# Hybrid decoder block on one core: the second matmul of the indexer scores contracts over all 128 partitions instead of 64

## The chip, the core and the metric

The kernel runs on one core of one Trainium2 chip. The metric is device time in microseconds (us), the median over runs of the whole program. A core has a matrix engine (PE, which loads a stationary operand, recorded as PEld, and then streams a moving operand past it), a vector engine (DVE), a scalar engine (ACT), GpSimd (POOL) and a sync engine (SP) that here issues most DMAs.

## The reference

One decoder layer on 256 tokens plus 16 learned meta tokens, width 1024, all in float32. Cut to what the change touches:

```python
proj = rmsnorm(h, norm_mix_g) @ w_in          # split into q, k, v, qi, ki, wi, cu, cb, cc, ga, gb
...
rel   = relu(einsum('bthd,bsd->bths', qi_b, k_idx))            # 8 index heads, each 64 wide
score = einsum('bths,bth->bts', rel, w_b * IDX_SCALE)
score = where(visible, score, -inf)
_, sel = top_k(score, topk)                                     # 68 keys for each token
...                                                             # attention over the selected keys
y_conv = (cb * short_conv(cc * cu, conv_w)) @ w_conv_out
mixed  = sigmoid(ga) * y_attn + sigmoid(gb) * y_conv
h = h + mixed @ w_out
...                                                             # SwiGLU FFN, final norm
```

The index scores only choose keys: `rel` for 8 heads, weighted and added up, then the top 68.

## The kernel before

**Numbers in two parts.** Every float32 operand of a matmul is split into a high part in the PE's reduced float32 format and a low part, the rest. A product is made of three terms: high by high, high by low and low by high. ACT makes the high part of a weight block (`whi`, line 137), DVE the low part (`wlo`, line 145).

**Weights.** The weights come as 160 blocks of 128 x 1024 in the order in which they are used (`UNITS`); each is loaded, split some four blocks ahead (`ahead`), and multiplied by one of two helpers. `narrow` makes three matmuls for each of 8 slices of a block (lines 214 to 216, 256 to 272 columns). `product` makes two for each slice: one of 512 columns that takes the high weights by high and low activations at once (line 250), and one of 256 for the low weights (line 253). Both write to a PSUM buffer named `acc`, of which there are four.

**Index scores.** The index queries of a head are 64 wide. `indexer_queries` puts the high part of head 2j into partitions 0 to 63 and its low part into 64 to 127 of `qi`; for head 2j+1 the high part is in 64 to 127 and the low part in 0 to 63. The keys' high part `ki.hi` and low part `ki.lo` stand in both halves of the partitions. A score of one head is then two matmuls into a `misc` buffer (four of these): one over 128 partitions that adds high by high and low by high, and one over the 64 partitions where the high part of the query stands, by the keys' low part. `scores` is called for 2 blocks of 128 tokens by 8 heads, 16 times in all: 8 times with 144 columns (the keys that the first token block can see) and 8 times with 272. After each, ACT applies relu (line 306) and DVE adds the weighted result up (lines 310 and 312).

**Order.** The order on every engine is that of the code. `some_scores` takes two scores at a time and is called after the matmuls of the short convolution's blocks (`cu`, `cb`, `cc`): eight groups of two scores, that is of four matmuls, each between two weight blocks. Then the eight attention heads follow, whose `logits` (line 370) are made with the same three-pass helper of 144 and 272 columns, into `misc` buffers too, over 128 partitions throughout. In the rows, `qi` goes by the name of its buffer, `big`, and the attention's q and k by `q_hi`, `q_lo`, `k_hi`, `k_lo`.

Of the kernel before, what the change touches and what calls it, by code (L numbers as in the profile page):

```python
# [25 lines left out]
DI = 64  # L26
# [42 lines left out]
def program(nc, tc, h_in, params, weights, out):  # L69
# [14 lines left out]
    mm = nc.tensor.matmul  # L84
# [3 lines left out]
    def bank():  # L88
        return acc.tile([P, 512], F32, name="acc")

    def side():
        return misc.tile([P, 512], F32, name="misc")

    def temp(n=L):
        t = ring.tile([P, L], F32, name="temp")
        return t[:, 0:n]
# [121 lines left out]
    def narrow(i, src, c0=0, late=False):  # L218
        n = src.hi.shape[2]
        o = bank()[:, 0:n - c0]  # L220
        hi, lo = got.pop(i)
        w = lambda k: slice(k * P, k * P + P)
        for k in range(KT):
            xh, xl = src.hi[:, k, c0:n], src.lo[:, k, c0:n]
            if late:
                mm(o, hi[:, w(k)], xh, start=k == 0, stop=False)
                mm(o, hi[:, w(k)], xl, start=False, stop=False)
            else:
                three_passes(o, hi[:, w(k)], lo[:, w(k)], xh, xl, k == 0, k == KT - 1)
        if late:  # L230
            for k in range(KT):
                mm(o, lo[:, w(k)], src.hi[:, k, c0:n], start=False, stop=k == KT - 1)
        return o
# [21 lines left out]
    def product(i, src, c0=0):  # L255
        o = bank()
        hi, lo = got.pop(i)
        w = lambda k: slice(k * P, k * P + P)
        for k in range(KT - 1):
            wide_high(o, hi[:, w(k)], src, k, c0, start=k == 0, stop=False)  # L260
            wide_low(o, lo[:, w(k)], src, k, c0, start=False, stop=False)
        k = KT - 1
        wide_low(o, lo[:, w(k)], src, k, c0, start=False, stop=False)
        wide_high(o, hi[:, w(k)], src, k, c0, start=False, stop=True)
        return o

    bias = one.tile([P, OFF[1] + L], F32, name="bias")
    qi = one.tile([P, NI, S], R, name="big2")
# [3 lines left out]
    ki = Pair(one, [P, L], "ki")  # L272
# [25 lines left out]
    def scores(t, head):  # L298
        n = SEEN[t]
        o = side()  # L300
        c = slice(t * P, t * P + P)
        rows = slice((head % 2) * DI, (head % 2) * DI + DI)
        mm(o[:, 0:n], qi[:, head, c], ki.hi[:, 0:n], start=True, stop=False)  # L303
        mm(o[:, 0:n], qi[rows, head, c], ki.lo[rows, 0:n], start=False, stop=True)  # L304
        r = temp(n)
        act(r, o[:, 0:n], AF.Relu)
        s = sc[:, OFF[t]:OFF[t] + n]
        w = wsc[:, t, head:head + 1]
        if head == 0:
            V.tensor_scalar(s, r, w, None, op0=OP.mult)  # L310
        else:
            V.scalar_tensor_tensor(s, r, w, s, op0=OP.mult, op1=OP.add)
# [209 lines left out]
    def some_scores():  # L522
        for _ in range(2):
            if tasks:
                t, head = tasks.pop(0)
                scores(t, head)
                if head == NI - 1:
                    causal(t)
                    steps.extend([topk_steps(t)] * (-(-TOPK // 8) + 1))
# [45 lines left out]
    o = narrow(0, uT, late=True)  # L575
# [3 lines left out]
    last, o = o, narrow(1, uT, late=True)  # L579
# [4 lines left out]
    last, o = o, narrow(2, uT)  # L584
# [3 lines left out]
    last, o = o, narrow(3, uT)  # L588
# [3 lines left out]
    for i in range(4, LEAD):  # L592
        last, o = o, narrow(i, uT)
# [5 lines left out]
        n = LEAD - 4  # L599
# [28 lines left out]
    for j in range(KT):  # L628
        i = first["wo"] + j
        ahead(i)  # L630
        o = product(i, mix()) if j < KT - 1 else narrow(i, mix())
# [31 lines left out]
    for j in range(KT):  # L663
        o = bank()
# [36 lines left out]
    for n in range(2):  # L701
        c = slice(n * 512, n * 512 + 512)
# [53 lines left out]
```

## Time and profile before

| | |
|---|---|
| median of 3 runs | 504.36 us (504.21 to 505.34) |
| span of the profiled execution | 502.3 us |
| its own time beside its span | not listed apart; the median is 2.06 us above the span |
| PE busy | 492.7 us, 98% of the span |
| PE weight loads (PEld) busy | 444.5 us, 88% |
| DVE, ACT, POOL busy | 72%, 60%, 15% |
| mean granted PE clock | 0.998 of full |

The span reaches from the first to the last instruction. PE and PEld are the same engine: a load of the next stationary operand can run under a matmul. Matmuls are pipelined and their ends are modelled, so durations of neighbours overlap; the distance from the start of one to the start of the next is what a matmul takes of the engine.

### The profile page before, as it was taken

What the parts mean: (1) busy time and instruction counts of PE and PEld (TensorE: products, weight loads), DVE (VectorE), ACT (ScalarE), POOL (GpSimd) and SP (SyncE); (2) the same over time, 40 slices, a digit from 0 to 9 for tenths busy, and PEclk for the clock granted to TensorE, in tenths of its full rate; (3) what the DMA queues carried; (4) which work ended last, traced back from release to release, by engine and by line L of the source; (5) the groups of instructions that cost most, each with busy time, mean ns of one, the idle gap of its engine ahead of it and who ended that gap; (6) DMA issues with size and microseconds to landing.
All of it is one profiled execution on the core that took longest, in us unless ns stands there. A gap on an engine that the chain in (4) does not pass through costs nothing.

```text
span 502.3 us, 8349 instructions
## 1 busy us (share of the span) xinstructions
PE 492.7 (98%) x3157; PEld 444.5 (88%) x3157; DVE 362.7 (72%) x661; ACT 301.9 (60%) x567; POOL 73.3 (15%) x75
## 2 busy tenths in 40 slices
PE   8999999999999999999999999999999999999995
PEld 6988889999999999888888989888888888888895
DVE  5898678886677777587776797778777777764521
ACT  6685566655577777765656465666666656553511
POOL 3451112211000000000000012121221122000110
PEclk9999999999999999999999999999999999999999
DMA  8847335556434544365556475456656565665002
GB/s 311 322 129 251 127 127 185 193 169 215 163 127 127 159 135 133 124 204 197 182 176 201 133 246 176 155 187 201 203 178 197 173 196 182 206 204 177 1 0 85
DMA packets 24376, 86.09 MB, mean 171 GB/s; under 512 B 2832, under 2 KB 2832, under 8 KB 24336
## 3 DMA queue, kind: packets, MB, share of 16 engines
q1 hardware_dynamic: 24192, 85.54, 51.6%
q8 instruction: 25, 0.41, 0.3%
q14 instruction: 15, 0.12, 0.1%
q10 hardware_dynamic: 144, 0.02, 0.0%
HBM read 84.50 MB, written 1.05 MB: 170 GB/s over the span
## 4 chain that ended last, share of the span: by engine, by line
PE 90%; issue 3%; DVE 2%; ACT 1%; DMA 1%; POOL 1%; SPq 0%; POOLq 0%; DVEq 0%
PE acc L250 42%; PE acc L253 21%; PE acc L214 7%; PE acc L215 7%; PE acc L216 7%; DMA h_all<-in_h_in_dram 1%; PE misc L304 1%; DVE aT L566 1%; PE misc L303 1%; PE misc L410 1%; ACT temp L555 0%; PE misc L427 0%; PE misc L216 0%; POOL rt L201 0%; PE misc L214 0%
## 5 line engine op out<-in xcount | busy, mean ns | idle before, releaser
L250 PE MATMUL acc<-aT,whi 128*128 128x512 f32 x576 | 202.7, 399 | 0.0
L145 DVE TENSOR_TENSOR wlo<-raw,whi 128x1024 fp32r<-128x1024 f32 x158 | 192.8, 1225 | 7.0 <-ACT whi L137 4.8
L137 ACT ACTIVATE whi<-raw 128x1024 fp32r<-128x1024 f32 x158 | 163.8, 1047 | 0.4 <-PE acc L250 0.3
L253 PE MATMUL acc<-aT,wlo 128*128 128x256 f32 x576 | 150.1, 281 | 0.0
L250 PEld LDWEIGHTS acc<-aT,whi 128*128 128x128 f32 x576 | 105.3, 188 | 19.7
L250 PE MATMUL acc<-big,whi 128*128 128x512 f32 x330 | 115.2, 394 | 0.0
L253 PEld LDWEIGHTS acc<-aT,wlo 128*128 128x128 f32 x576 | 108.8, 189 | 5.7
L253 PE MATMUL acc<-big,wlo 128*128 128x256 f32 x330 | 88.4, 282 | 0.0
L215 PE MATMUL acc<-aT,whi 128*128 128x272 f32 (+2 forms) x272 | 78.1, 287 | 1.1 <-DVE aT L566 1.1
L214 PE MATMUL acc<-aT,whi 128*128 128x272 f32 (+2 forms) x272 | 78.6, 289 | 0.0
L216 PE MATMUL acc<-aT,wlo 128*128 128x272 f32 (+2 forms) x272 | 77.6, 285 | 0.0
L246 DVE TENSOR_TENSOR temp<-acc,temp 128x256 f32<-128x256 f32 x87 | 36.9, 424 | 49.8 <-ACT temp L245 49.8
L250 PEld LDWEIGHTS acc<-big,whi 128*128 128x128 f32 x330 | 60.6, 188 | 11.9
L253 PEld LDWEIGHTS acc<-big,wlo 128*128 128x128 f32 x330 | 62.0, 188 | 2.5
L215 PEld LDWEIGHTS acc<-aT,whi 128*128 128x128 f32 x272 | 51.3, 189 | 1.8 <-DVE aT L566 1.3
L214 PEld LDWEIGHTS acc<-aT,whi 128*128 128x128 f32 x272 | 51.4, 189 | 0.7
L216 PEld LDWEIGHTS acc<-aT,wlo 128*128 128x128 f32 x272 | 51.2, 188 | 0.0
L119 ACT ACTIVATE big<-temp 128x256 fp32r<-128x256 f32 x45 | 18.8, 418 | 47.0 <-DVE temp L660 23.2
L623 POOL TENSOR_TENSOR sq_sum<-sq_sum,temp 128x256 f32<-128x256 f32 x12 | 11.0, 918 | 236.6 <-ACT temp L620 236.6
L245 ACT ACTIVATE temp<-acc 128x256 f32<-128x256 f32 x87 | 32.7, 376 | 13.9 <-PE acc L250 11.5
L656 POOL TENSOR_TENSOR temp<-temp,rstd 128x256 f32<-128x256 f32 x22 | 26.0, 1182 | 93.9 <-ACT temp L655 93.9
L239 DVE TENSOR_TENSOR h_all<-h_all,acc 128x256 f32<-128x256 f32 x16 | 6.7, 416 | 28.6 <-PE acc L250 21.7
(162 smaller groups left out, 529.5 us busy)
## 6 DMA issues: line engine op xcount, KB each, us to landing
raw<-in_weights_dram SPq DMA_DIRECT2D x158, 512.0 KB, 3.5
h_all<-in_h_in_dram SPq DMA_DIRECT2D x4, 272.0 KB, 4.6
out_dram<-big SPq DMA_DIRECT2D x4, 256.0 KB, 2.3
raw<-in_weights_dram SPq DMA_DIRECT2D x2, 256.0 KB, 3.8
par<-in_params_dram ACTq DMA_DIRECT2D x1, 24.0 KB, 3.3
```

Source lines behind the costliest of these rows:

```text
L119: act(hi, src, AF.Copy)
L137: act(high[i], raw[i], AF.Copy)
L145: V.tensor_sub(lo, raw.pop(i), high[i].bitcast(F32))
L214: mm(o, wh, xh, start=first, stop=False)
L215: mm(o, wh, xl, start=False, stop=False)
L216: mm(o, wl, xh, start=False, stop=last)
L245: act(t, o[:, S:2 * S], AF.Copy)
L246: V.tensor_tensor(t, o[:, 0:S], t, OP.add)
L250: mm(halves(o), w, src.both[:, k, :, c0:c0 + S], **kw)
L253: mm(o[:, 0:S], w, src.hi[:, k, c0:c0 + S], **kw)
L623: G.tensor_tensor(sq_sum, sq_sum, sq, OP.add)
L656: G.tensor_tensor(s, s, rstd, OP.mult)
```

## The change

The second matmul of a score takes all 128 partitions: the stationary operand is now the whole `qi[:, head, c]` (query high and low part), and the moving one the keys' low part in both halves. The result gains the term low by low, which was left out before. The stationary operand is then the same as that of the first matmul of the pair. Nothing else changes: on every engine the list of instructions, their order and their semaphore waits are the same as before.

```diff
@@ -299,9 +299,8 @@
         n = SEEN[t]
         o = side()
         c = slice(t * P, t * P + P)
-        rows = slice((head % 2) * DI, (head % 2) * DI + DI)
         mm(o[:, 0:n], qi[:, head, c], ki.hi[:, 0:n], start=True, stop=False)
-        mm(o[:, 0:n], qi[rows, head, c], ki.lo[rows, 0:n], start=False, stop=True)
+        mm(o[:, 0:n], qi[:, head, c], ki.lo[:, 0:n], start=False, stop=True)
         r = temp(n)
         act(r, o[:, 0:n], AF.Relu)
         s = sc[:, OFF[t]:OFF[t] + n]
```

## Rows read from the trace of the kernel before

**Rows 1.** The page: busy us, share, instructions; the chain that ended last, by engine.

```profile
PE 492.7 (98%) x3157; PEld 444.5 (88%) x3157; DVE 362.7 (72%) x661; ACT 301.9 (60%) x567; POOL 73.3 (15%) x75
...
PE 90%; issue 3%; DVE 2%; ACT 1%; DMA 1%; POOL 1%; SPq 0%; POOLq 0%; DVEq 0%
```

**Rows 2.** What PE waited for from 34 to 480 us: total, times, longest.

```profile
PE acc L215 <- DVE aT L566: 1.1, 1, 1.1
```

**Rows 3.** Windows: length, busy us of PE, PEld, DVE, ACT, POOL, granted clock, DMA.

```profile
20.00:35.00 15.00, 13.51 (x111) 13.06 (x110) 12.87 (x21) 10.39 (x17) 10.38 (x9) 1.00 0.49 158
41.50:71.00 29.50, 29.50 (x180) 24.75 (x179) 20.83 (x45) 17.38 (x37) 5.43 (x7) 1.00 0.47 160
71.00:120.00 49.00, 49.00 (x370) 47.28 (x370) 42.49 (x95) 30.16 (x55) 11.91 (x12) 1.00 0.55 175
```

**Rows 4.** Line 304 on PE: min/median/max ns, first and last start us, forms.

```profile
L304 PE MATMUL misc<-ki_lo,big x16: 330/359/389, 41.9 to 70.7; 64*128 64x144 f32 x8, 64*128 64x272 f32 x8
```

**Rows 5.** Timeline of PE, a group of scores with 144 columns: start us, us.

```profile
45.65 0.23 PE L303 MATMUL misc<-ki_hi,big 128*128 128x144 f32 x1
45.81 0.33 PE L304 MATMUL misc<-ki_lo,big 64*128 64x144 f32 x1
46.07 0.34 PE L303 MATMUL misc<-ki_hi,big 128*128 128x144 f32 x1
...
46.59 0.39 PE L214 MATMUL acc<-aT,whi 128*128 128x258 f32 x1
46.82 0.29 PE L215 MATMUL acc<-aT,whi 128*128 128x258 f32 x1
46.94 0.29 PE L216 MATMUL acc<-aT,wlo 128*128 128x258 f32 x1
```

**Rows 6.** Timeline of PE, a group of scores with 272 columns.

```profile
57.39 0.28 PE L303 MATMUL misc<-ki_hi,big 128*128 128x272 f32 x1
57.60 0.39 PE L304 MATMUL misc<-ki_lo,big 64*128 64x272 f32 x1
57.92 0.39 PE L303 MATMUL misc<-ki_hi,big 128*128 128x272 f32 x1
...
58.56 0.39 PE L214 MATMUL acc<-aT,whi 128*128 128x258 f32 x1
58.78 0.28 PE L215 MATMUL acc<-aT,whi 128*128 128x258 f32 x1
```

**Rows 7.** Timeline of PE, the logits of one attention head.

```profile
125.97 0.23 PE L214 MATMUL misc<-k_hi,q_hi 128*128 128x144 f32 x1
126.04 0.27 PE L215 MATMUL misc<-k_lo,q_hi 128*128 128x144 f32 x1
126.15 0.27 PE L216 MATMUL misc<-k_hi,q_lo 128*128 128x144 f32 x1
126.26 0.33 PE L214 MATMUL misc<-k_hi,q_hi 128*128 128x272 f32 x1
126.43 0.28 PE L215 MATMUL misc<-k_lo,q_hi 128*128 128x272 f32 x1
126.55 0.29 PE L216 MATMUL misc<-k_hi,q_lo 128*128 128x272 f32 x1
126.67 0.27 PE L394 MATMUL misc<-ident,temp 128*128 128x128 f32 x1
```

**Rows 8.** Timeline of the weight loads, at the scores and at the logits.

```profile
45.80 0.18 PEld L304 LDWEIGHTS misc<-ki_lo,big 64*128 64x128 f32 x1 [0.20 <-issue]
46.07 0.19 PEld L303 LDWEIGHTS misc<-ki_hi,big 128*128 128x128 f32 x1
...
125.97 0.19 PEld L215 LDWEIGHTS misc<-k_lo,q_hi 128*128 128x128 f32 x1
```

**Rows 9.** Timelines of DVE and PE: the 88th `wlo` (first of two), and its first use.

```profile
286.28 2.35 DVE L145 TENSOR_TENSOR wlo<-raw,whi 128x1024 fp32r<-128x1024 f32 x2
...
293.05 0.28 PE L253 MATMUL acc<-big,wlo 128*128 128x256 f32 x1
```

## The prediction

> **What bounds the kernel now.** I read the page first: PE is busy for 98% of the span, and the chain that ended last runs over PE for 90% of it [rows 1]. A busy PE row alone proves little, because the records of neighbouring matmuls overlap; so next I asked what PE waited for. From 34 us to 480 us there is one such wait, 1.1 us in all, and it belongs to the first units after the input norm [rows 2]. After it PE goes from matmul to matmul without a gap: in the stretch with the index scores, 41.5 to 71 us, it is busy for all of its 29.5 us, and in the stretch behind it for all of 49 us, at the full granted clock [rows 3]. So in this kernel the time from one matmul's start to the next one's start is time on the path, wherever it stands before 480 us, as long as the weights keep coming.
>
> The changed matmul is the 64-partition one of the scores: 16 of them, 8 of 144 columns and 8 of 272 [rows 4], all between 41.9 and 71 us. They come in eight groups of four matmuls (303, 304, 303, 304), four groups of each width.
>
> **What a group costs now.** I read starts, not durations. In a group of 144 columns the first matmul starts at 45.65, and then come 45.81, 46.07, and the next weight block's first matmul at 46.59: steps of 0.16, 0.26, and 0.52 for the last two, so 0.26 each. That first matmul of the next block again takes 0.23 until 46.82, while its twins after it take 0.12 [rows 5]. From 45.65 to 46.82 it is 1.17 us. In a group of 272 columns the steps are 0.21, 0.32, then 0.64 for two, and 0.22 for the next block's first: 57.39 to 58.78 is 1.39 us [rows 6].
>
> These steps are not the price of streaming. The difference between the two widths, 128 columns, costs 0.32 - 0.26 = 0.06 us; about 0.2 us of each step remains that no column explains. Nor is PE waiting for another engine there [rows 2]. What it does show is a load that cannot be prepared: the 64-row load of line 304 begins at 45.80, when its matmul begins at 45.81, after 0.20 us of idle on the load side, and the 128-row load after it begins at 46.07, again only with its own matmul [rows 8, 5]. So both directions, 128 to 64 rows and back, put load, stream and a gap one behind the other.
>
> **What a group will cost.** The trace of before holds the same thing without a change of height: the logits of one head, three matmuls of 144 and three of 272 columns, into the same kind of buffer, with the same stationary operand twice in a row, 128 rows throughout. There the load of the second matmul begins at 125.97, exactly when the first one starts streaming [rows 7, 8]. The starts go 125.97, 126.04, 126.15, 126.26, then for 272 columns 126.43, 126.55, and 126.67 for what follows [rows 7]: 0.70 us for six. That divides into 0.11 for each of 144 columns (0.07, which only says that the first load was ready, then 0.11 and 0.11) and 0.125 for each of 272, since 3 x 0.11 + 3 x 0.125 = 0.705. After the change all four matmuls of a group are of this kind, and the next block's first matmul takes its usual 0.12 [rows 5].
>
> - 144 columns: 4 x 0.11 + 0.12 = 0.56 instead of 1.17, 0.61 saved in a group.
> - 272 columns: 4 x 0.125 + 0.12 = 0.62 instead of 1.39, 0.77 saved.
> - Eight groups: 4 x 0.61 + 4 x 0.77 = 5.5 us.
>
> Three of the groups are followed by a `product`, whose first matmul has 512 columns instead of some 258; its own excess I take to be the same 0.11. The first group, whose 64-row matmuls begin at 41.9 [rows 4], follows two small transposes, and its first load may still come late; that is one step of at most 0.26 - 0.11 = 0.15 that may not be saved, which I leave in the range.
>
> **What is not saved or added.** The number of instructions is the same on every engine, loads included, so nothing is gained from the fact that a pair now uses one stationary operand twice; the logits show such a pair reloading it. The added contraction over 64 more partitions costs no columns. The matmul reads the second half of `ki_lo` too, but the waits on every engine are the same as before.
>
> **Where the saving could stop.** It reaches the end only if the weights are there 5.5 us earlier. The thinnest cushion that I found after 42 us is at the 88th `wlo`: the first of two that begin at 286.28 takes some 1.2, about half of 2.35, so it ends at 287.5, and PE first uses it at 293.05 [rows 9]: 5.55 us. It does not have to give all of that up, since DVE works behind PE in program order and moves forward with it. In the score stretch itself DVE has 20.83 us of work [rows 3]; in 29.5 - 5.5 = 24.0 us that is 87% busy, which is just what it is in the stretch behind, 42.49 of 49 us [rows 3], where PE never waits. ACT would have 17.38 of 24.0, 72%. So I let the whole 5.5 us through. The page's own time beside the span is not given; the median stands 2.06 us above the span of 502.3, and I take that as fixed: span 496.8, time 504.36 - 5.5 = **498.9 us**.
>
> **Bounds of the step.** The nearest rows give an interval for a step after the change: for 144 columns 0.07 (the logits' first) to 0.16 (the step from 303 to 304 now, its load being ready), for 272 columns 0.12 to 0.21 [rows 5 to 7]. The cheap end makes a group 4 x 0.07 + 0.12 = 0.40 and 4 x 0.12 + 0.12 = 0.60, and saves 4 x (1.17 - 0.40) + 4 x (1.39 - 0.60) = 6.2 us, 498.1; the dear end makes it 0.76 and 0.96 and saves 4 x (1.17 - 0.76) + 4 x (1.39 - 0.96) = 3.4 us, 501.0. I stand at 0.11 and 0.125, since the logits match in rows, columns, buffer and repeated operand.
>
> **Rivals.**
>
> *Loads stop hiding.* If a 128-row load could not run under a 128-row matmul, a step would be load plus stream: 0.11 + 0.06 = 0.17 for 144 columns (0.06 is what 128 columns cost above), and 0.11 + 0.12 = 0.23 for 272. Against the 1.17 and 1.39, with the usual 0.12 behind, that saves 4 x (1.17 - 0.80) + 4 x (1.39 - 1.04) = 2.9 us: 501.5. The logits' loads speak against it [rows 8], and so does the usual step of 0.12 [rows 5], which is shorter than such a sum. The Trainium skill states this rule: its page "TensorE: Matmul & The Clock Gate", section "Part 3: Packing small matmuls — row/col tiling", says that weight loads overlap with matmuls in flight only when their row groups differ, and its closing table advises cutting contractions of under 128 into row groups, which is what the old matmul did and the new one undoes. By that rule the time would be the 501.5 just given; the trace does not agree, since a 128-row load begins at 125.97 under a 128-row matmul that starts at 125.97. Chance 2%.
>
> *The feed gives part of it back.* If DVE or the loads of weights have less room than I read, PE meets a wait after 71 us and loses between 1 and 5 of the 5.5: 500 to 504. The cushion of 5.55 us and the 87% speak against it; chance 6%, two thirds of it still faster by more than 0.2%.
>
> *The height is not the cause.* If the 0.2 us hang on something else that the scores have and the logits lack (two matmuls to a buffer instead of three to half of one, or `qi` as the stationary operand), the steps remain and so does the time, 504.4. For the height speaks that line 303 behind 304 is as late as 304 itself though it is a plain 128-row matmul. Chance 3%.
>
> *Slower: a wait that lowers the clock.* If PE, being earlier, ran dry for so long that its clock fell to the lower level, each weight block would take twice as long. A block of 24 matmuls at 0.12 [rows 5] takes 2.9 us and would lose as much, so from two such blocks on (5.8 us) the change loses. Against it: from 20 to 35 us PE was idle for 1.5 of 15 us, and the granted clock stayed at 1.00, the 2.4 GHz level [rows 3]. Chance 2%.
>
> **How the numbers follow.** The likeliest case keeps 87%. A change under 0.2%, about 1 us, could not be told from none by a measurement of this kernel. Faster by more than that: 87 + 2 + 4 = 93%; within it: the 3% of the third rival and 2% of the second, 5%; slower: 2%. The range is that of the step's bounds, 498.1 to 501.0, opened by 0.1 at the low end for the spread of runs; it leaves out the rivals and little else.
>
> **What would show it.** In the profile after, the second matmul of a score stands as 128*128; the steps in a group are 0.11 to 0.13, its load begins with the matmul before it, and the block behind a group has no long first step. The stretch from the first score to the last shrinks by about 5 us, relu on ACT waits for PE less, and every later stage stands 5.5 us earlier with no new wait of PE. I am wrong in the size if the steps stay near 0.16 and 0.21, wrong in the cause if they stay at 0.26 and 0.32, and wrong about the path if the steps shrink but PE then waits for `wlo` or `whi` after 71 us.

## The result and the profile after

| | before | after |
|---|---|---|
| median, all runs compared | 504.85 us (504.21 to 505.34, 4 runs) | 498.64 us (498.46 to 499.88, 4 runs) |
| ratio to before, 95% interval | | 0.9886 [0.9867, 0.9905] |
| span of the profiled execution | 502.3 us | 496.8 us |

The forecast was 498.9 us, with a span of 496.8 us. The interval of the ratio puts the gain between 4.8 and 6.7 us. The runs of before fall into two bands (504.2 to 504.4, and 505.3) and one of the changed kernel's lies 1.2 us above its other three, so the 6.2 us between the medians mixes bands; within the lower band the difference is 5.7 us, within the upper one 5.5.

The page of the changed kernel, its line of busy times, which answers to [rows 1]:

```profile
PE 487.0 (98%) x3157; PEld 442.7 (89%) x3157; DVE 362.3 (73%) x661; ACT 300.3 (60%) x567; POOL 73.4 (15%) x75
```

PE does as many matmuls and loads as before, and is still busy for 98% of a span that is 5.5 us shorter. The other engines' work is what it was. The five waits of PE that its view lists over the whole span are single ones, as before; this is one of the two longest, which answers to [rows 2] (none of the other four is in the score stretch):

```profile
PE acc L215 <- DVE aT L565: 1.1, 1, 1.1
```

No wait is new; two of the others grew by 0.3 us each, and one shrank by 0.2. Windows of the same kernel, columns as in [rows 3], the score stretch and 49 us of the stretch behind:

```profile
41.50:66.40 24.90, 24.90 (x186) 23.68 (x186) 20.61 (x45) 15.02 (x36) 4.20 (x6) 1.00 0.58 191
...
71.00:120.00 49.00, 49.00 (x370) 47.29 (x370) 42.06 (x91) 30.83 (x56) 11.15 (x10) 1.00 0.59 186
```

In the score stretch PEld's share rises from 24.75 of 29.5 to 23.68 of 24.9 us: the time in which no load ran falls from 4.75 to 1.2 us. (This window reaches a little further into the block behind, which is why it holds 186 matmuls and not 180; over the whole span the loads are as many as before.) The stretch behind is as full as it was.

The ends of the score stretch, its first matmul and the second one of the block behind the last group, in the kernel before (with the second score matmul) and in the changed one, whose first score matmul, at 41.88, stands among the lines of the small transposes below:

```profile
41.68 0.33 PE L303 MATMUL misc<-ki_hi,big 128*128 128x144 f32 x1
41.95 0.33 PE L304 MATMUL misc<-ki_lo,big 64*128 64x144 f32 x1
...
71.21 0.28 PE L215 MATMUL acc<-aT,whi 128*128 128x258 f32 x1
```

```profile
65.86 0.28 PE L215 MATMUL acc<-aT,whi 128*128 128x258 f32 x1
```

It takes 65.86 - 41.88 = 23.98 us instead of 71.21 - 41.68 = 29.53, which is 5.55 us less.

Timeline of PE in the changed kernel, a group of 144 columns and a group of 272, to be laid beside [rows 5, 6] (the lines after the removed one have moved up by one, so 302 and 303 are the former 303 and 304):

```profile
45.25 0.23 PE L302 MATMUL misc<-ki_hi,big 128*128 128x144 f32 x1
45.31 0.28 PE L303 MATMUL misc<-ki_lo,big 128*128 128x144 f32 x1
45.42 0.28 PE L302 MATMUL misc<-ki_hi,big 128*128 128x144 f32 x1
45.53 0.28 PE L303 MATMUL misc<-ki_lo,big 128*128 128x144 f32 x1
45.65 0.33 PE L214 MATMUL acc<-aT,whi 128*128 128x258 f32 x1
45.81 0.28 PE L215 MATMUL acc<-aT,whi 128*128 128x258 f32 x1
...
55.16 0.29 PE L302 MATMUL misc<-ki_hi,big 128*128 128x272 f32 x1
55.28 0.29 PE L303 MATMUL misc<-ki_lo,big 128*128 128x272 f32 x1
55.41 0.29 PE L302 MATMUL misc<-ki_hi,big 128*128 128x272 f32 x1
55.53 0.29 PE L303 MATMUL misc<-ki_lo,big 128*128 128x272 f32 x1
55.66 0.28 PE L214 MATMUL acc<-aT,whi 128*128 128x258 f32 x1
55.78 0.29 PE L215 MATMUL acc<-aT,whi 128*128 128x258 f32 x1
```

From the group's first matmul to the second one of the next block it is 45.81 - 45.25 = 0.56 us instead of 1.17, and 55.78 - 55.16 = 0.62 instead of 1.39. The weight loads show why; a load of the first group:

```profile
45.25 0.19 PEld L303 LDWEIGHTS misc<-ki_lo,big 128*128 128x128 f32 x1
```

Line 303's load begins at 45.25, with the matmul ahead of it, and not with its own as at 45.80 in [rows 8].

### The profile page after: what moved, and what is told of

The parts are those of the page before. It is cut to its first block, busy times and chain, and to the rows that moved or that the text cites. A ratio compares the mean times of both kernels' runs of the same rounds, so it can differ in the third digit from the quotient of the medians.

```text
span 496.8 us, 8349 instructions
## 1 busy us (share of the span) xinstructions
PE 487.0 (98%) x3157; PEld 442.7 (89%) x3157; DVE 362.3 (73%) x661; ACT 300.3 (60%) x567; POOL 73.4 (15%) x75
## 4 chain that ended last, share of the span: by engine, by line
PE 90%; issue 3%; DVE 2%; ACT 1%; DMA 1%; POOL 1%; SPq 0%; POOLq 0%; DVEq 0%
PE acc L250 42%; PE acc L253 22%; PE acc L215 7%; PE acc L216 7%; PE acc L214 7%; DMA h_all<-in_h_in_dram 1%; DVE aT L565 1%; PE misc L409 1%; ACT temp L554 0%; PE misc L426 0%; PE misc L302 0%; POOL rt L201 0%; PE misc L214 0%; ACT whi L137 0%; PE misc L216 0%
```

## The experiments

Times of these runs stand beside runs of the kernel before on the same chip: 504.79 us (504.03 to 505.62, 13 runs) for the first three and for that with the same matmul elsewhere, 504.45 us (503.86 to 505.76, 13 runs) for the other three. The nine profiled executions also differ for a reason outside the scores. In four of them (before, changed, the first two experiments) the first score matmul begins between 41.5 and 41.9 us, and the mean granted clock of PE from 8 to 16 us is 1.00; in the other five it begins between 42.2 and 42.7, and that clock is 0.79, with 0.50, the 1.2 GHz level, from 11 to 12 us. In all nine PE is busy for only 0.38 to 0.43 us of the one from 8 to 9. So the group lengths of the traces decide where a time alone would not.

**Half as many changes of height, as many 64-row matmuls.** On the kernel before:

```diff
-        mm(o[:, 0:n], qi[:, head, c], ki.hi[:, 0:n], start=True, stop=False)
-        mm(o[:, 0:n], qi[rows, head, c], ki.lo[rows, 0:n], start=False, stop=True)
+        os = [side() for _ in heads]
+        for o, head in zip(os, heads):
+            mm(o[:, 0:n], qi[:, head, c], ki.hi[:, 0:n], start=True, stop=False)
+        for o, head in zip(os, heads):
+            rows = slice((head % 2) * DI, (head % 2) * DI + DI)
+            mm(o[:, 0:n], qi[rows, head, c], ki.lo[rows, 0:n], start=False, stop=True)
...
```

> The kernel before, with the four matmuls of a group reordered: both heads' 128-row matmuls first, then both heads' 64-row matmuls. As many 64-row matmuls as before (16), half as many changes of height (2 in a group instead of 4). Theory, the price hangs on a change of height: before a group cost 0.61 (144 columns) or 0.77 us (272) more than without any change, so 0.15 or 0.19 for each change; two of them are saved in each of eight groups, 4 x 0.31 + 4 x 0.39 = 2.8 us, which makes 502 us where the kernel before takes 504.4 to 504.9. Rival, the price hangs on each 64-row matmul (its load or its stream is slow): 16 of them remain, the time stays at that of the kernel before. Second rival, two 64-row matmuls in different halves of the array run at the same time: then the second one costs next to nothing and the gain is up to 0.12 us in a group larger, 501 us.

Measured 500.69 us (500.12 to 501.47), ratio 0.9920 [0.9905, 0.9936]. Timeline of PE, a group of 272 columns:

```profile
55.56 0.41 PE L303 MATMUL misc<-ki_hi,big 128*128 128x272 f32 x2
55.90 0.39 PE L306 MATMUL misc<-ki_lo,big 64*128 64x272 f32 x2
56.22 0.39 PE L214 MATMUL acc<-aT,whi 128*128 128x258 f32 x1
56.44 0.28 PE L215 MATMUL acc<-aT,whi 128*128 128x258 f32 x1
```

Its loads of 64 rows:

```profile
55.90 0.19 PEld L306 LDWEIGHTS misc<-ki_lo,big 64*128 64x128 f32 x2
```

The group takes 56.44 - 55.56 = 0.88 us instead of 1.39. The 16 matmuls of 64 rows are all there, so the price does not hang on each of them; the first rival falls. The second one is also seen: both 64-row matmuls together take 56.22 - 55.90 = 0.32 us, the step that a single one took in [rows 6]. One lies in partitions 0 to 63, the other in 64 to 127, and they run at once: both records fit into the 0.39 us, and both loads into the 0.19 us, that one alone takes. So of the 0.51 us that the group saves, 0.12 is this and 0.39 the two changes of height, 0.19 each, as the theory had it. The Trainium skill's page "TensorEngine Tiling (Array Packing)", section "Key Properties", says both things, that different tiles run in parallel and that a change of the tiling mode drains the engine; it gives no price. The trace agrees with the first; for the second it shows a price at each change, but not that this is a drain.

**Another stationary operand.** On the changed kernel:

```diff
-        mm(o[:, 0:n], qi[:, head, c], ki.lo[:, 0:n], start=False, stop=True)
+        mm(o[:, 0:n], qi[:, (head + 1) % NI, c], ki.lo[:, 0:n], start=False, stop=True)
```

> The changed kernel, but the second matmul of a pair takes the query of the next head as its stationary operand, over 128 partitions, so that the two matmuls of a pair no longer share one. It computes another low term than the reference's. Theory, the height alone matters: as the changed kernel, 498.6 us, steps of 0.11 and 0.125 us in a group. Rival, the gain comes from using one stationary operand twice: the steps grow by the part that this gave, up to the 0.26 and 0.32 of before, and the time goes up to 504 us.

Measured 499.12 us (498.39 to 499.36), ratio 0.9886 [0.9871, 0.9900]. Timeline of PE, a group of 272 columns:

```profile
54.82 0.29 PE L302 MATMUL misc<-ki_hi,big 128*128 128x272 f32 x1
...
55.44 0.28 PE L215 MATMUL acc<-aT,whi 128*128 128x258 f32 x1
```

0.62 us for the group, as in the changed kernel. That a pair now shares an operand gives nothing.

**96 rows.** On the changed kernel; part of the low term is left out:

```diff
-        mm(o[:, 0:n], qi[:, head, c], ki.lo[:, 0:n], start=False, stop=True)
+        mm(o[:, 0:n], qi[0:96, head, c], ki.lo[0:96, 0:n], start=False, stop=True)
```

> The second matmul over 96 partitions (0 to 95) instead of 128, so that part of the low term is left out for every second head. Theory, the price is for a change of the array's height between 64 and the full one, and 96 rows run at the full one: as the changed kernel, 498.6 us, steps of 0.11 and 0.125 us. Rival, any operand with fewer than 128 rows than its neighbours pays: near the kernel before, 504 us, steps of 0.26 and 0.32 us.

Measured 499.16 us (498.49 to 499.61), ratio 0.9888 [0.9872, 0.9905].

```profile
55.55 0.29 PE L302 MATMUL misc<-ki_hi,big 128*128 128x272 f32 x1
55.68 0.29 PE L303 MATMUL misc<-ki_lo,big 96*128 96x272 f32 x1
...
56.18 0.28 PE L215 MATMUL acc<-aT,whi 128*128 128x258 f32 x1
```

The group takes 0.63 us. An operand of 96 rows between neighbours of 128 is free; that it has fewer rows than they have is not what costs.

**32 rows.** The same with `qi[0:32, head, c]` and `ki.lo[0:32, 0:n]`; most of the low term is left out.

> The second matmul of a score over 32 partitions (0 to 31), so that most of the low term is left out. Theory, a change of the array's height puts a gap and an unhidden load between two matmuls whatever the smaller height is: the steps in a group stay at 0.26 and 0.32 us and the time at 504.4 to 504.9 us, as the kernel before with 64 rows. Rival, fewer rows are cheaper in the load or in the gap: shorter steps than with 64 rows, 499 to 503 us.

Measured 504.71 us (503.86 to 505.57, 10 runs), ratio 1.0000 [0.9988, 1.0011].

```profile
58.12 0.28 PE L302 MATMUL misc<-ki_hi,big 128*128 128x272 f32 x1
58.33 0.38 PE L303 MATMUL misc<-ki_lo,big 32*128 32x272 f32 x1
58.65 0.39 PE L302 MATMUL misc<-ki_hi,big 128*128 128x272 f32 x1
...
59.50 0.28 PE L215 MATMUL acc<-aT,whi 128*128 128x258 f32 x1
```

Steps of 0.21 and 0.32, as in [rows 6], and 59.50 - 58.12 = 1.38 us for the group, where it was 1.39. A change to 32 rows costs what one to 64 does.

**The same matmul elsewhere.** On the changed kernel, in the output projection; half of the sum of two slices is left out in 7 blocks:

```diff
-            wide_low(o, lo[:, w(k)], src, k, c0, start=False, stop=False)
+            if UNITS[i][0] == "wo" and k in (2, 5):
+                mm(o[:, 0:S], lo[0:DI, w(k)], src.hi[0:DI, k, c0:c0 + S], start=False, stop=False)
+            else:
+                wide_low(o, lo[:, w(k)], src, k, c0, start=False, stop=False)
```

> The changed kernel, with 64-row matmuls put elsewhere: in the output projection, in 7 blocks, two of the 256-column matmuls by the low weights take 64 partitions instead of 128 (they leave out half of the sum of these two slices). No instruction more. Theory, a change of height costs wherever PE is on the path: 14 such matmuls with two changes each, at 0.15 to 0.19 us a change, 14 x 0.30 to 0.38 = 4.2 to 5.3 us more than the changed kernel, 503 to 504 us, with the steps around each 64-row matmul longer by that. Rival, the price belonged to the scores (their buffers, their operand): no more than the changed kernel, 498.6 us.

Measured 504.65 us (503.88 to 505.53, 10 runs), ratio 0.9998 [0.9988, 1.0007]: 14 matmuls with fewer rows give the whole gain back. Timeline of PE around one of them, and below it the same four matmuls in the changed kernel:

```profile
288.85 0.40 PE L250 MATMUL acc<-big,whi 128*128 128x512 f32 x1
289.18 0.38 PE L262 MATMUL acc<-big,wlo 64*128 64x256 f32 x1
289.49 0.50 PE L250 MATMUL acc<-big,whi 128*128 128x512 f32 x1
289.83 0.40 PE L253 MATMUL acc<-big,wlo 128*128 128x256 f32 x2
```

```profile
285.96 0.40 PE L250 MATMUL acc<-big,whi 128*128 128x512 f32 x1
286.20 0.28 PE L253 MATMUL acc<-big,wlo 128*128 128x256 f32 x1
286.32 0.40 PE L250 MATMUL acc<-big,whi 128*128 128x512 f32 x1
286.55 0.28 PE L253 MATMUL acc<-big,wlo 128*128 128x256 f32 x1
```

289.83 - 288.85 = 0.98 us against 286.55 - 285.96 = 0.59: 0.39 for one, 14 x 0.39 = 5.5 us. That is a little above the 4.2 to 5.3 expected. (The spans differ by 502.9 - 496.8 = 6.1 us, of which about 0.6 is the later first score.) The rival, that the price belongs to the scores, falls.

**The small transposes at full height.** On the changed kernel, the two transposes of the indexer weights over 128 partitions and columns (the multiplication ahead of them and the copy behind, both on DVE, are widened to match and are left out here):

```diff
-            nc.tensor.transpose(o[:, t * NI:t * NI + NI], wT[:, t * P:t * P + P], ident[rows, rows])
+            nc.tensor.transpose(o[:, t * P:t * P + P], wT[:, t * P:t * P + P], ident)
...
```

> The changed kernel with its last change of height ahead of the scores removed: the two transposes of the indexer weights take all 128 partitions and 128 columns instead of 8 by 8. In the changed kernel, from the last matmul of the block ahead to the second matmul of the first score it is 0.21 + 0.22 + 0.17 = 0.60 us (41.45 to 42.05). Theory: steps of 0.11 to 0.12 at full height although the transposes are 16 times as wide, 0.12 + 0.11 + 0.11 + 0.11 = 0.45 us, 0.15 less; in the time, 498.5 instead of 498.6 us, which only the trace can tell. Rival, small matmuls are the cheaper ones: the four steps come to 0.60 us or more.

Measured 499.32 us (499.21 to 499.87), ratio 0.9898 [0.9877, 0.9918], not to be told from the changed kernel by its time. Timeline of PE in the changed kernel, and below it here:

```profile
41.45 0.28 PE L216 MATMUL acc<-aT,wlo 128*128 128x258 f32 x1
...
41.88 0.34 PE L302 MATMUL misc<-ki_hi,big 128*128 128x144 f32 x1
42.05 0.27 PE L303 MATMUL misc<-ki_lo,big 128*128 128x144 f32 x1
```

```profile
42.30 0.28 PE L216 MATMUL acc<-aT,wlo 128*128 128x258 f32 x1
42.42 0.38 PE L286 MATMUL misc<-ident,temp 128*128 128x128 f32 x2
42.55 0.31 PE L300 MATMUL misc<-ki_hi,big 128*128 128x144 f32 x1
42.70 0.28 PE L301 MATMUL misc<-ki_lo,big 128*128 128x144 f32 x1
```

0.40 us instead of 0.60: transposes with 16 times the rows and columns are the cheaper ones here, by 0.20 us where 0.15 were expected. The step of the first score itself hardly changes (0.15 us instead of 0.17).

**Four heads at a time.** The first experiment with four heads in a group, at every second call; the edit is otherwise that one's.

> The kernel before with the scores taken four heads at a time: four 128-row matmuls, then four 64-row ones in alternating halves of the array, at every second call. Two changes of height for four heads. From the run with two heads at a time: a group of 144 columns there takes 0.757 us; two more 128-row matmuls (0.22) and one more pair of 64-row ones that runs at once (0.11) make 1.09, and with 272 columns 0.885 + 0.25 + 0.125 = 1.26; the changed kernel needs 2 x 0.564 - 0.12 = 1.01 and 2 x 0.618 - 0.12 = 1.12 for four heads. Theory, the two changes cost a little more than running two at once gives back: 2 x 0.08 + 2 x 0.14 = 0.4 us more than the changed kernel, 499.1 us. Rival, the second pair of 64-row matmuls cannot load under the first and waits 0.2 us too: 499.9 us. Second rival, fewer groups are cheaper than that, and this order beats the changed kernel: under 498.4 us.

Measured 500.44 us (499.49 to 500.92), ratio 0.9915 [0.9894, 0.9935]. Timeline of PE, the first group and one of 272 columns:

```profile
42.70 0.56 PE L303 MATMUL misc<-ki_hi,big 128*128 128x144 f32 x3
43.84 0.33 PE L303 MATMUL misc<-ki_hi,big 128*128 128x144 f32 x1 [0.58 <-DVE wsc L289]
...
56.94 0.66 PE L303 MATMUL misc<-ki_hi,big 128*128 128x272 f32 x4
57.53 0.52 PE L306 MATMUL misc<-ki_lo,big 64*128 64x272 f32 x4
57.98 0.39 PE L214 MATMUL acc<-aT,whi 128*128 128x258 f32 x1
58.20 0.28 PE L215 MATMUL acc<-aT,whi 128*128 128x258 f32 x1
```

The four loads of 64 rows in the latter:

```profile
57.53 0.30 PEld L306 LDWEIGHTS misc<-ki_lo,big 64*128 64x128 f32 x4 [0.15 <-issue]
```

The group of 272 columns takes 58.20 - 56.94 = 1.26 us, the forecast length, where the changed kernel needs 1.12 for four heads. On top comes a wait that I had not reckoned with: the fourth matmul of the first group needs a fourth `misc` buffer, which still holds the transposed weights until DVE has copied them, 0.58 us; 43.84 - 42.70 = 1.14 us for three steps instead of some 0.35. That explains some 0.8 of the 1.3 us by which the time lies above the expected 499.1; in the profiled execution the first score also begins 0.8 us later than in the changed kernel's (42.70 against 41.88). Both rivals fall, by the group and not by the time: the second pair does load in time, all four loads being done 0.30 us after the first began, and the order does not beat the changed kernel.

## Why the prediction was right

- **PE's starts are the path.** Right. The stretch from the first score to the block behind the last group is 5.55 us shorter, of which the eight groups, counted as above, make 5.53, and no new wait appeared. The span is 502.3 - 496.8 = 5.5 us shorter because the first score begins 0.20 us later and what stands behind is some 0.15 us shorter.
- **A group of 144 columns would take 0.56, one of 272 columns 0.62 us.** Measured 0.56 and 0.62. The logits of [rows 7] were the right pattern.
- **The sum of 5.5 us.** Right in the mechanism: 5.55 us in the score stretch. That the span hits the forecast to the tenth is in part luck, since the 0.20 and 0.15 us outside the scores nearly cancel. The median of before used for the forecast was 504.36, and 0.49 us higher with a fourth run.
- **The first group might save one step less.** It did not. Its first step is still late, 42.05 - 41.88 = 0.17 us where the group at 45.25 has 0.06; but it was as late before, 41.95 - 41.68 = 0.27 where the group at 45.65 had 0.16, so nothing of the saving was lost. Full transposes leave it at 0.15, so the height of the 8-row ones is not what makes it late.
- **The weights would come in time.** Right. Timelines of DVE and PE in the changed kernel, the same pair as in [rows 9]:

```profile
280.84 2.35 DVE L145 TENSOR_TENSOR wlo<-raw,whi 128x1024 fp32r<-128x1024 f32 x2
...
287.61 0.28 PE L253 MATMUL acc<-big,wlo 128*128 128x256 f32 x1
```

  Both stand 5.44 us earlier than before, so the distance of 6.77 us between them is unchanged: DVE moved forward with PE, as argued, and the cushion was not touched. The rival of a weaker feed (6%) did not come.
- **Loads stop hiding** (2%): refuted by the load at 45.25 under a matmul that starts then. The Trainium skill's rule in "TensorE: Matmul & The Clock Gate", section "Part 3: Packing small matmuls — row/col tiling", that loads overlap only when the row groups differ, does not hold for these full-height matmuls; the same section also allows a load into the background weight buffer, and no trace here shows which buffer a load goes to.
- **The height is not the cause** (3%): refuted by the experiments with 96 and 32 rows, with another operand, and elsewhere in the program.
- **A wait that lowers the clock** (2%): did not come; the granted clock stays at 1.00 in the score stretch and the one behind. Such a fall does occur in this program, but ahead of the scores: in five of the nine profiled executions the clock is 0.50 from 11 to 12 us.

What the price is made of can be read in part. A matmul whose load was ready takes 0.21 us when a change follows (57.39 to 57.60 in [rows 6]) and 0.12 to 0.13 when none does: 0.09 more. A matmul behind a change, with none after it, takes 0.22 instead of 0.12 (58.56 to 58.78): 0.10 more. Together they are the 0.19 us for a change. The second part goes with a load that begins only with its own matmul, and is near the 0.11 us of the load-bound steps; that the load is all of it is argued. What the first part is stays open, since the rows of PE, whose ends are modelled, show no gap there. That the array runs empty is what the Trainium skill's page "TensorEngine Tiling (Array Packing)", section "Key Properties", calls it; these traces do not show it.

## What to carry to other kernels

In a stream of matmuls that PE runs without a gap, look at the distances between starts, and at the weight loads that begin together with their own matmul: there the load was not prepared. A contraction over 64 or 32 partitions between full-height neighbours cost 0.15 to 0.2 us for each change here, and two transposes of 8 rows together 0.20 us more than full ones; filling the operand to 96 or 128 partitions, even with terms that nobody needs, was free. Running half-height matmuls two at once gives back about 0.12 us for each pair of 272 columns and costs two changes, 0.39 us, for each group; the two pairs of four heads were not enough (1.26 against 1.12 us). That more pairs would be is not shown.

## What was not expected of the hardware

Two 64-row matmuls in different halves of the partitions and different buffers take the time of one, 0.32 us for both, inside an otherwise full-height program. Between 9 and 11 us, behind one us in which PE was busy for some 0.4, its granted clock falls to the lower level in five of the nine profiled executions and not in the other four, though the programs are the same up to there; the lower clock goes with a first score 0.4 to 1.2 us later. A 96-row operand runs like a 128-row one (steps of 0.12 and 0.13 us), and a 32-row one costs what a 64-row one does (1.38 against 1.39 us for the group), so among these four heights the price comes in classes and not with the row count.
